# Unit 1's weights prepared in steps 1 to 5, the last unit's gates of five tiles given in its last three steps, and the sample's lane begun at the second output slot

## The chip, the cores and the metric

One Trainium2 chip, one of its cores. The metric is the device time of one execution in microseconds (us). The engines of the core are PE (TensorE, matmuls), DVE (VectorE), ACT (ScalarE), POOL (GpSimd) and SP (SyncE, which here only issues DMAs). Each takes its instructions in the order in which the program lists them for it, and an instruction that waits holds up what is listed behind it on its engine.

## What is computed

One layer of a streaming encoder: 2048 prompt rows (16 tiles of 128) and 128 sample rows (8 streams of 16) of width 1024 are normed and modulated to h; h times `w_in` gives queries, keys, values and two groups of gates; differential attention (softmax, 4 heads) and stick-breaking attention (8 heads) run side by side; their outputs are gated, projected, merged and projected again.

```python
def merge_branches(oa, ob, za, zb, ga, gb, subln_g, lam_init, w_branch_a, w_branch_b, w_out):
    b, s = oa.shape[:2]
    oa = rms_norm(oa, subln_g) * (1.0 - lam_init)
    ya = (oa.reshape(b, s, WIDTH_A) * jax.nn.silu(za)) @ w_branch_a
    yb = (ob.reshape(b, s, WIDTH_B) * jax.nn.silu(zb)) @ w_branch_b
    return (jax.nn.sigmoid(ga) * ya + jax.nn.sigmoid(gb) * yb) @ w_out
...
        h, gate = adaln_modulate(xp, c_prompt, norm_g[l], w_ada[l], b_ada[l])
        qa, ka, va, za, qb, kb, vb, zb, ga, gb = project_inputs(h, w_in[l], pos_p)
...
        xp = xp + gate * merge_branches(oa, ob, za, zb, ga, gb, subln_g[l], lam_init,
                                        w_branch_a[l], w_branch_b[l], w_out[l])
```

The sample rows do the same against a cache of 512 older keys and values. The new keys and values are outputs too.

## The kernel before

**Units, tiles, steps.** The heads are worked off in eight units. An even unit is one softmax head, an odd unit a pair of stick-breaking heads. Every unit goes over 17 tiles, the sample's tile (`NT`) first and then prompt tiles 0 to 15, so there are 136 steps `(u, t)`. All products that need more than half precision are made of f16 halves: h and each weight are cut into a high and a low half, and three matmuls stand for one.

**The main loop** (`for n in range(len(steps) + 2)`) gives the work of a step: score chunks of the step's tile against its keys (two matmuls of 128x512, L697 and L698), what ACT, DVE and POOL do to them (softmax for even units; for odd units the scan L671, which DVE runs over 512 columns at a time and the next chunk continues), the transposes of the weights by DMA (L615, issued on SP, into `wt`), and the products with the values (L754 to L759). Beside that stand pieces of the **projection line**, taken by `take(target)`: the projections run about five steps ahead of the scores (`LEAD`). `project` gives 24 matmuls L461 for a tile, and in the odd units 24 gate matmuls L537 more, all into the one bank "t" of PSUM; ACT takes the result out (L540) and SP stores it in `g_d`. The gate matmuls read the tile's h, which lies in one of three buffers `hs[0..2]` that `fetch_h` (L438) fills in turn from `hT_d`.

**Side pieces** of a step: `back`, the next unit's weights (`prepare_unit`: raw loads, sums of squares on ACT L295, a bound, then `cut` and `gate_cut` into halves, L315 on ACT or L317 on POOL and L320 on DVE); `spare`, sums of squares of the branch weights, the output weight and the cached values (a load of 512 KB and one L295 each); `cached`, keys of the cache. Unit 1 is the first one with gates. Its weights were begun at step 3 of unit 0.

**Early work** (`early_work`, from the end of the line on): the branch weights, then the inputs of the first two output tiles (`first`): o and z rows loaded into `hs[0]` and `hs[1]` (L1291, L1292), multiplied, cut into halves into `hs[2]` (L315, L320) and transposed on PE (L1281, taken out by ACT L1282).

**The output phase** has a slot n for each of the 17 tiles in the order 0 to 14, sample, 15, and two more. Slot n runs the branch projection L1471 of its n-th tile (48 matmuls) and the output projection L1508 of the tile before it (48), and prepares the tile after it. Beside them stands the **sample's lane**, the attention of the sample rows against their cache in 52 pieces, spread by `aside(n)` over the first 13 slots: loads `dc`, cast on ACT into `v16c` (L315), scores L849, weights through DMA into `dwt`, and L872.

A list scheduler orders the instructions of each engine from this program; those marked `kept` stay where the program has them.

## Time and profile before

| | us |
|---|---|
| median of 3 runs | 2244.19 |
| range of the runs | 2240.26 to 2244.84 |
| the profiled execution | 2238.37 |
| its span (first to last instruction) | 2236.6 |

The profiled execution's own time is 1.8 us above its span and 5.8 us below the median of the runs. In the span the main loop begins at about 130 us, its last score chunk is done at about 1774 us, and the output phase runs from about 1782 us to the end. The views used below are: the page (busy time of each engine), a table of windows (busy time of each engine in stretches of the span, with `PEclk`, the mean TensorE clock that was granted, 1.00 being full speed), groups of equal instructions (count, busy time, mean duration in ns, idle time of the engine just before them and what ended it), waits (what ended the idle time of an engine), and the timeline (start, duration, instruction, and in brackets the idle time ahead of it and its releaser). `PEld` is the loading of weights into the array, which overlaps PE.

### The profile page before, as it was taken

What the parts mean: (1) busy time and instruction counts of PE and PEld (TensorE: products, weight loads), DVE (VectorE), ACT (ScalarE), POOL (GpSimd) and SP (SyncE); (2) the same over time, 40 slices, a digit from 0 to 9 for tenths busy, and PEclk for the clock granted to TensorE, in tenths of its full rate; (3) what the DMA queues carried; (4) which work ended last, traced back from release to release, by engine and by line L of the source; (5) the groups of instructions that cost most, each with busy time, mean ns of one, the idle gap of its engine ahead of it and who ended that gap; (6) DMA issues with size and microseconds to landing.
All of it is one profiled execution on the core that took longest, in us unless ns stands there. A gap on an engine that the chain in (4) does not pass through costs nothing. (4 is left out here: it accounts for less than half of the span.)

```text
span 2236.6 us, 41454 instructions
## 1 busy us (share of the span) xinstructions
PE 2068.9 (93%) x14608; PEld 1115.8 (50%) x14608; DVE 1747.9 (78%) x3799; ACT 1606.9 (72%) x3212; POOL 700.4 (31%) x608
## 2 busy tenths in 40 slices
PE   5998999999999999999999998999998689999997
PEld 3654555555555455555544554555554334444443
DVE  4657868889887788988778888787778868888864
ACT  3967877789887778987677788876577666676531
POOL 1122014446420343752024356301334512211210
PEclk8999999999999999999999999999999699999999
DMA  9777768889797989978879899675667899899762
GB/s 331 257 247 177 168 153 208 198 212 208 194 248 163 226 205 199 213 209 215 198 191 222 187 219 207 188 165 130 148 154 170 168 254 267 230 247 241 194 170 66
DMA packets 824672, 450.00 MB, mean 201 GB/s; under 512 B 556081, under 2 KB 763233, under 8 KB 823950
## 3 DMA queue, kind: packets, MB, share of 16 engines
q1 hardware_dynamic: 823514, 446.96, 80.9%
q8 instruction: 114, 1.87, 0.3%
q14 instruction: 96, 0.79, 0.1%
q10 hardware_dynamic: 948, 0.39, 0.1%
HBM read 228.82 MB, written 86.02 MB: 141 GB/s over the span
## 5 line engine op out<-in xcount | busy, mean ns | idle before, releaser
L677 POOL TENSOR_TENSOR sc_p<-sc_p,sc_n 128x127 f32<-128x127 f32 (+7 forms) x192 | 313.2, 1634 | 663.9 <-DVE sc_n L671 514.1
L461 PEld LDWEIGHTS <-hs 128*128 128x128 f16 x3120 | 292.2, 98 | 312.4 <-issue 4.3
L461 PE MATMUL ps_mm<-wa,hs 128*128 128x512 f16 x1590 | 383.8, 380 | 1.5 <-DVE v L320 0.9
L461 PE MATMUL ps_mm<-wb,hs 128*128 128x512 f16 x1530 | 379.7, 379 | 1.0 <-DVE qbuf L496 1.0
L537 PE MATMUL ps_t<-wb,hs 128*128 128x512 f16 x1224 | 291.8, 379 | 3.2 <-DVE qst L565 2.9
L671 DVE TENSOR_TENSOR_SCAN sc_n<-ps_s,sc_n,zero_t 128x512 f32<-128x512 f32 x192 | 245.4, 1278 | 36.0 <-ACT ps_s L131 30.7
L697 PE MATMUL ps_s<-k,qst 128*128 128x512 f16 (+3 forms) x640 | 224.2, 351 | 38.8 <-DVE sc_n L671 26.8
L608 DVE TENSOR_TENSOR sc_n<-sc_p,sc_n 128x128 f16<-128x128 f32 (+7 forms) x192 | 221.8, 1157 | 39.7 <-ACT sc_n L605 39.2
L537 PEld LDWEIGHTS <-hs 128*128 128x128 f16 x1632 | 154.7, 98 | 182.6 <-DVE qst L565 7.3
L131 ACT ACTIVATE sc_p<-ps_s,usc 128x512 f32<-128x512 f32 (+3 forms) x320 | 203.2, 635 | 36.2 <-PE ps_s L698 22.6
L698 PE MATMUL ps_s<-k,qst 128*128 128x512 f16 (+3 forms) x640 | 225.0, 352 | 0.0
L605 ACT CAST sc_n<-sc_p 128x128 f16<-128x128 f32 (+7 forms) x192 | 154.8, 807 | 63.8 <-POOL sc_p L677 63.0
L131 ACT ACTIVATE ps_s<-ps_s,usc 128x512 f32<-128x512 f32 (+3 forms) x320 | 195.5, 611 | 0.0
L758 PE MATMUL ps_o<-v,wt 128*128 128x128 f16 x1088 | 135.5, 226 | 22.5 <-DMA wt<-sc_n 22.5
L1508 PE MATMUL ps_o<-wo,wb 128*128 128x512 f16 x624 | 142.3, 384 | 0.8 <-ACT wb L1282 0.8
L591 DVE TENSOR_SCALAR_CACHE_REDUCE sc_p<-ps_s,usc 128x512 f32<-128x512 f32 (+3 forms) x160 | 106.1, 664 | 31.8 <-PE ps_s L698 17.5
L758 PEld LDWEIGHTS <-wt 128*128 128x128 f16 x1088 | 103.1, 102 | 51.3 <-DMA wt<-sc_n 28.5
L759 PE MATMUL ps_o<-v,wt 128*128 128x64 f16 x1088 | 127.8, 199 | 0.0
L1517 POOL TENSOR_TENSOR x<-m,x 128x512 f32<-128x512 f32 x32 | 48.1, 1504 | 251.2 <-DVE m L1512 164.5
L671 DVE TENSOR_TENSOR_SCAN sc_n<-ps_s,zero_t 128x128 f32<-128x128 f32 (+3 forms) x128 | 104.2, 814 | 23.8 <-ACT ps_s L131 23.0
L502 POOL TENSOR_TENSOR rot<-pr,rope 128x256 f32<-128x256 f32 x68 | 56.7, 833 | 205.5 <-ACT pr L475 109.9
L754 PE MATMUL ps_o<-v,wt 128*128 128x128 f16 x544 | 101.5, 224 | 19.2 <-DMA wt<-sc_n 19.0
(379 smaller groups left out, 4547.9 us busy)
## 6 DMA issues: line engine op xcount, KB each, us to landing
hs<-hT_d SPq DMA_DIRECT2D x130, 512.0 KB, 4.6
g_d<-gt SPq DMA_DIRECT2D x68, 256.0 KB, 3.3
out_dram<-pr SPq DMA_DIRECT2D x204, 64.0 KB, 3.6
wa<-in_w_in_dram SPq DMA_DIRECT2D x34, 256.0 KB, 5.7
o_d<-o SPq DMA_DIRECT2D x136, 64.0 KB, 2.2
wa<-g_d SPq DMA_DIRECT2D x17, 512.0 KB, 4.7
wb<-g_d SPq DMA_DIRECT2D x17, 512.0 KB, 4.9
hs<-o_d SPq DMA_DIRECT2D x17, 512.0 KB, 4.5
```

Of the source, the lines that this page charges most:

```text
L131: i = S.activation(**kw)
L461: T.matmul(box["p"], box["h"][:, hi, k, :], U["w"][k][:, wi, :], start=(n == 0), stop=(n == 3 * KT - 1))
L537: T.matmul(box["g"][:, 0:gw], box["h"][:, hi, k, :], U["wg"][k // per][:, k % per, wi, :], start=(j == 0), stop=(j == 3 * KT - 1))
L605: x = S.copy(out=hi, in_=src)
L608: V.tensor_tensor(out=lo, in0=src, in1=hi, op=ALU.subtract)
L671: V.tensor_tensor_scan(out=dst[:, lo : lo + n][:, ::-1], data0=src[:, 0:n][:, ::-1], data1=zero_t[:, 0:1].to_broadcast([P, n]), initial=fi ...
L677: G.tensor_tensor(out=p[:, 0:m], in0=p[:, 0:m], in1=n[:, 1 : m + 1], op=ALU.mult)
L697: T.matmul(p[:, 0:n], qst[:, c, :], kk[:, c, 0:n], start=True, stop=False)
L698: T.matmul(p[:, 0:n], qst[:, 2 + c, :], kk[:, c, 0:n], start=False, stop=not diag)
L758: T.matmul(po[:, c * P : (c + 1) * P], wt[:, wj, :], vt[:, c, :, :], start=first, stop=False)
L759: T.matmul(po[:, c * P : c * P + 64], wt[:, nb + wj, :], vt[:, c, 0, :], start=False, stop=last)
L1508: T.matmul(po, st["y"][:, yi * 8 + k, :], wo[j * 4 + k // 2][:, wi, k % 2, :], start=(n == 0), stop=(n == 3 * KT - 1))
```

## The change

1. `prepare_unit(1)` begins at step 1 instead of 3, and its pieces are spread so that they end with step 5 instead of step 10. No sum of squares of `spare` is made in unit 0 any longer (nine were, in its last nine steps); they are made in unit 6.
2. The gate matmuls of tiles 11 to 15 of unit 7, the last one (5 x 24), leave the projection line. They are given as 60 pieces of two matmuls in the last three steps, in the order of tiles 13, 15, 14, 11, 12. The h of tiles 13, 14 and 15 is still in the three buffers; that of tiles 11 and 12 is loaded again, one after the other into `hs[2]`. `early_work` begins with the last two steps, where before it began as soon as the line was empty.
3. The sample's lane begins at slot 1; from there the 52 pieces are spread over 12 slots.
4. The output gate rows of the sample's tile come from `gate_rows(1, j)` (a load of 9x512 and one small matmul into bank "t") ahead of their multiplication; before, all were loaded at once and two matmuls L1503 put them into banks ahead of the tile's L1508. The norm and the store of the last two output tiles are given a little later in their slots.

```diff
--- before.py
+++ after.py
@@ -59,6 +59,9 @@
 H_AT = 2
 Q_BUFS = 6
 TR_AFTER = 5
+LATE, CUTS_AT = 5, 2
+LATE_ORDER = (NT - 3, NT - 1, NT - 2, NT - 5, NT - 4)
+LATE_SHARE = (0, 20, 20, 20)
 LEAD = 5.0
 TILE_TIME = 0.6
 SAMPLE_TIME = 0.3
@@ -431,6 +434,9 @@
         G.memset(qb[:, 1, :, 1, :], 0.0)
     silu_z = {}
     at_hand, ahead, fetched = {}, {}, []
+
+    def late(u, t):
+        return u == 7 and NT - LATE <= t < NT
 
     def fetch_h(u, t):
         ahead[u, t] = hs[len(fetched) % 3].bitcast(F16).rearrange("p (f k n) -> p f k n", f=2, n=P)
@@ -534,13 +540,18 @@
             for j in range(per * n, per * n + per):
                 hi, wi = ((0, 0), (0, 1), (1, 0))[j % 3]
                 k = j // 3
-                T.matmul(box["g"][:, 0:gw], box["h"][:, hi, k, :], U["wg"][k // per][:, k % per, wi, :], start=(j == 0), stop=(j == 3 * KT - 1))
+                x = T.matmul(box["g"][:, 0:gw], box["h"][:, hi, k, :], U["wg"][k // per][:, k % per, wi, :], start=(j == 0), stop=(j == 3 * KT - 1))
+                if late(U["u"], t) and j == per * n:
+                    kept(x)
             if per * n + per == 3 * KT:
                 gt = gts[:, 0:512]
-                S.activation(out=gt[:, 0:gw], in_=box["g"][:, 0:gw], func=AF.Identity, scale=sc[:, 6:7])
+                x = S.activation(out=gt[:, 0:gw], in_=box["g"][:, 0:gw], func=AF.Identity, scale=sc[:, 6:7])
+                if late(U["u"], t):
+                    kept(x)
                 load(out=g_d[t][:, g0 : g0 + gw], in_=gt[:, 0:gw])
 
-        return [lambda n=n: piece(n) for n in range(12)] + [lambda n=n: gate_piece(n) for n in range(3 * KT // per if gw else 0)]
+        U["gates", t] = box, [lambda n=n: gate_piece(n) for n in range(3 * KT // per if gw else 0)]
+        return [lambda n=n: piece(n) for n in range(12)] + ([] if late(U["u"], t) else U.pop(("gates", t))[1])
 
     def transpose_qk(U, t):
         g, i = t // 4, t % 4
@@ -986,7 +997,22 @@
                 fetch_h(*steps[m + 1])
             made[i]()
 
-        return [lambda i=i: piece(i) for i in range(12 + 3 * GATES[u][1] // 128)]
+        return [lambda i=i: piece(i) for i in range(12 + (0 if late(u, t) else 3 * GATES[u][1] // 128))]
+
+    def late_gates(t):
+
+        def piece(i):
+            box, made = units[7]["gates", t]
+            if i == 0 and t < NT - 3:
+                box["h"] = ahead[8, t]
+            made[i]()
+            if i == len(made) - 1:
+                j = LATE_ORDER.index(t) + 1
+                if 3 <= j < len(LATE_ORDER):
+                    ahead[8, LATE_ORDER[j]] = x = hs[2].bitcast(F16).rearrange("p (f k n) -> p f k n", f=2, n=P)
+                    load(out=x, in_=hT_d[LATE_ORDER[j] // 4][:, LATE_ORDER[j] % 4, :, :, :])
+
+        return [lambda i=i: piece(i) for i in range(3 * GATES[7][1] // 128)]
 
     starts = []
     for m in range(len(steps)):
@@ -1015,7 +1041,7 @@
         return out
 
     def norm_at(u, t):
-        return u < 7 and t < NT and (t >= 7 if u == 0 else t >= 9 or u == 6)
+        return u < 7 and t < NT and (t >= 16 if u == 0 else t >= 9 or u == 6)
 
     def keys_at(u, t):
         return u in (1, 3, 5) and t < 8 or u in (2, 4, 6) and 9 <= t < 13
@@ -1266,6 +1292,7 @@
     branch_weights = list(range(8))
 
     L = {}
+    behind = [fn for t in LATE_ORDER for fn in late_gates(t)]
 
     def cut(dst, st, src, k, j, s, n):
 
@@ -1392,11 +1419,11 @@
         if n < len(steps):
             u, t = steps[n]
             past += duration(t)
-            if t == (3 if u == 0 else NT) and u < 7:
+            if t == (1 if u == 0 else NT) and u < 7:
                 back += prepare_unit(u + 1)
             if u == 7 and not back and not spare and not cached and len(branch_weights) > 1:
                 side.append((1.0, branch_weight))
-            for fn in back[: -(-len(back) // max(1, (W_READY if u else W_READY + 2) - t % NT))]:
+            for fn in back[: -(-len(back) // max(1, (W_READY if u else 6) - t % NT))]:
                 side.append((1.0, back.pop(0)))
             for todo, here in ((spare, norm_at), (cached, keys_at)):
                 if todo and here(u, t):
@@ -1407,11 +1434,18 @@
                 qk = scores(units[u], t, made)
         target = position(len(steps) * past / whole + LEAD)
         pieces = take(target, min(n + 1, len(steps) - 1))
-        if at[0] == len(line) and not pieces and not spare and not cached:
-            if cuts is None:
-                cuts = early_work()
-            pieces = [(1.0, fn) for fn in cuts[: -(-len(cuts) // (len(steps) + 2 - n))]]
-            del cuts[: len(pieces)]
+        if at[0] == len(line) and not spare and not cached:
+            m = n - len(steps)
+            if behind:
+                k = -(-len(behind) * LATE_SHARE[m] // sum(LATE_SHARE[m:]))
+                pieces += [(1.0, fn) for fn in behind[:k]]
+                del behind[:k]
+            if m >= -CUTS_AT:
+                if cuts is None:
+                    cuts = early_work()
+                k = -(-len(cuts) // (len(steps) + 2 - n))
+                pieces += [(1.0, fn) for fn in cuts[:k]]
+                del cuts[:k]
             if n == len(steps) + 1:
                 while due and due[0][2] == 0.0:
                     due.pop(0)[3]()
@@ -1455,10 +1489,6 @@
             T.matmul(pg, sel[0:9, :] if i else ones[0:1, :], gsm[0:m, :], start=True, stop=True)
             return pg
 
-        def rows_of_gates():
-            L["gsm"] = dec.tile([P, NB, P], F32, tag="dc", name="gsm", bufs=4).rearrange("p b n -> p (b n)")
-            load(out=L["gsm"][0:9, :], in_=gate_d)
-
         def branches(st):
 
             def half(j, br):
@@ -1498,9 +1528,6 @@
                     load(out=box["x"], in_=x_rows(t))
                 x = box["x"]
                 c = slice(j * 512, (j + 1) * 512)
-                if t == NT:
-                    pg = bank("ts"[j])
-                    T.matmul(pg, sel[0:9, :], L["gsm"][0:9, c], start=True, stop=True)
                 po = bank("o")
                 n = 0
                 for yi, wi in ((0, 0), (0, 1), (1, 0)):
@@ -1512,7 +1539,7 @@
                     V.scalar_tensor_tensor(out=m, in0=po, scalar=st["f"][:, 1:2], in1=gate[:, c], op0=ALU.mult, op1=ALU.mult)
                 else:
                     S.activation(out=m, in_=po, func=AF.Identity, scale=st["f"][:, 1:2])
-                    V.tensor_tensor(out=m, in0=m, in1=pg, op=ALU.mult)
+                    V.tensor_tensor(out=m, in0=m, in1=gate_rows(1, j), op=ALU.mult)
                 if t != tiles[-1]:
                     G.tensor_tensor(out=x[:, c], in0=m, in1=x[:, c], op=ALU.add)
                     return
@@ -1572,17 +1599,13 @@
                 side += [(IN_AT[i], stage) for i, stage in enumerate(stages)]
             if n + 1 <= NT:
                 side += [(2, lambda n=n: turned(states[tiles[n + 1]], n + 1 >= MOVED)), (4.5, lambda n=n: opened(states[tiles[n + 1]]))]
-            if n <= NT and tiles[n] == NT:
-                side.append((3.3, rows_of_gates))
-            if n > NT:
-                side += [(0.6, lambda n=n: normed_rows(tiles[n - 2], boxes[n - 2])), (1.1, lambda n=n: stored_rows(tiles[n - 2], boxes[n - 2]))]
-            elif n > 1:
+            if n > 1:
                 side += [(1, lambda n=n: normed_rows(tiles[n - 2], boxes[n - 2])), (2.5, lambda n=n: stored_rows(tiles[n - 2], boxes[n - 2]))]
             if n <= NT:
                 side.append((4.4 if MOVED <= n < NT else 7, lambda n=n: turned_y(states[tiles[n]], MOVED <= n < NT)))
             order = [(i, 0, cost, fn) for i, (cost, fn) in enumerate(work)] + [(at - 0.5, i + 1, 0.9 if at == 7 or at == 2 and n + 1 < MOVED else 0.1, fn) for i, (at, fn) in enumerate(side)]
             work = [(cost, fn) for _, _, cost, fn in sorted(order, key=lambda e: e[:2])]
-            interleave(work, aside(n))
+            interleave(work, aside(n) if n else [])
 
 
 # ---- launch: one core; inputs and outputs as the reference has them ----
```

How the instructions move, at three places. (The change adds lines to the program: its L323 is L320 of before, L318 is L315, L626 is L615, L1318 and L1319 are the loads L1291 and L1292.)

DVE, where the gate weights of unit 1 are cut (`wa`/`wb` are weight buffers, `sg` their scale, `sc_p` and `sc_n` the softmax weights of a score tile), before:

```order
L641 TENSOR_TENSOR r<-r,ls_i 128x1
L646 SCALAR_TENSOR_TENSOR sc_p<-sc_n,r,sc_p 128x1024
L320 SCALAR_TENSOR_TENSOR wa_174<-wb_1430,sg,wa_174 128x2x512
L320 SCALAR_TENSOR_TENSOR wa_173<-wb_1431,sg,wa_173 128x2x512
L646 SCALAR_TENSOR_TENSOR sc_p<-sc_n,r,sc_p 128x128
L320 SCALAR_TENSOR_TENSOR k_2341<-rot,sq_711,k_2341 128x2x64
L496 SCALAR_TENSOR_TENSOR qbuf_214<-rot,sq_711,qbuf_214 128x2x64
L591 TENSOR_SCALAR sc_p,mx<-ps_s,usc_702 128x512
L591 TENSOR_SCALAR sc_n,mx<-ps_s,usc_702 128x512
L320 SCALAR_TENSOR_TENSOR sc_n<-sc_p,r,sc_n 128x1024
L591 TENSOR_SCALAR sc_p,mx<-ps_s,usc_702 128x512
L320 SCALAR_TENSOR_TENSOR wb_1430<-wb_1432,sg,wb_1430 128x2x512
```

and in the change:

```order
L323 SCALAR_TENSOR_TENSOR wa_176<-wb_1430,sg,wa_176 128x2x512
L650 RECIPROCAL r<-l 128x2
L651 SCALAR_TENSOR_TENSOR r<-l,r,nlam 128x1
L323 SCALAR_TENSOR_TENSOR wa_175<-wb_1431,sg,wa_175 128x2x512
L652 TENSOR_TENSOR r<-r,ls_i 128x1
L657 SCALAR_TENSOR_TENSOR sc_p<-sc_n,r,sc_p 128x768
L323 SCALAR_TENSOR_TENSOR wa_174<-wb_1432,sg,wa_174 128x2x512
L323 SCALAR_TENSOR_TENSOR wa_173<-wb_1433,sg,wa_173 128x2x512
```

The four cuts stood among the scores of the ninth tile of unit 0 (1024 + 128 columns), two of them on either side of it; now all four stand at its sixth (768 columns).

SP, in the last steps of unit 7 (`hs` are the three buffers of h, `wt` the transposed weights that PE waits for, `g_d` the stored gates, `o_d` and `z_d` what the first output tile loads), before:

```order
L1291 DMA hs_180<-o_d_62 128x1024
L541 DMA g_d_111<-gt_1421 128x512
L615 DMA_TRANSPOSE wt<-sc_n 128x16x128
L748 DMA o_d_73<-o 128x128
L615 DMA_TRANSPOSE wt<-sc_n 128x12x128
L615 DMA_TRANSPOSE wt<-sc_n 128x16x128
L615 DMA_TRANSPOSE wt<-sc_n 128x12x128
L748 DMA o_d_74<-o 128x128
L615 DMA_TRANSPOSE wt<-sc_n 128x16x128
L615 DMA_TRANSPOSE wt<-sc_n 128x14x128
```

and in the change:

```order
L551 DMA g_d_109<-gt_1421 128x512
L1319 DMA hs_181<-z_d_79 128x512
L626 DMA_TRANSPOSE wt<-sc_n 128x16x128
L626 DMA_TRANSPOSE wt<-sc_n 128x12x128
L626 DMA_TRANSPOSE wt<-sc_n 128x16x128
L551 DMA g_d_111<-gt_1421 128x512
L1318 DMA hs_180<-o_d_62 128x1024
L759 DMA o_d_74<-o 128x128
L626 DMA_TRANSPOSE wt<-sc_n 128x14x128
L1013 DMA hs_182<-hT_d_59 128x2048
L551 DMA g_d_110<-gt_1421 128x512
L626 DMA_TRANSPOSE wt<-sc_n 128x16x128
```

From the store of the last tile's gates on there were only transposes and stores of o; now five stores of gates, the two loads of the first output tile and two loads of h (L1013) stand among the transposes.

ACT, at the third output tile (`hs<-hs,suy` is the cut of an output tile's inputs, `v16c<-dc` the cast of the sample's cached values, `wo` the output weights), before:

```order
L315 ACTIVATE wo_22622<-x,s_w_19830 128x1024
L1282 COPY wb_1426<-ps_s 128x1024
L295 ACTIVATE junk,usq<-hs_180 128x1024
L315 ACTIVATE v16c<-dc,s_c 128x8x128
L1477 CAST wa_174<-wa_169 128x512
L315 ACTIVATE v16c<-dc,s_c 128x8x128 x2
L131 ACT_TABLE_LOAD
L131 ACTIVATE dsc,l<-dsc,nm 128x640 x2
L1477 CAST wa_174<-wb_1429 128x512
L131 ACT_TABLE_LOAD
L131 ACTIVATE hs_181<-hs_181 128x512
L315 ACTIVATE hs_182<-hs_180,suy 128x1024
```

and in the change:

```order
L298 ACTIVATE junk,usq<-hs_180 128x1024
L318 ACTIVATE wo_22634<-x,s_w_19830 128x1024
L1507 CAST wb_1429<-wb_1431 128x512
L318 ACTIVATE hs_182<-hs_180,suy 128x1024
L318 ACTIVATE v16c<-dc,s_c 128x8x128 x3
```

The cut of that tile stood behind three casts and two rows of the sample's softmax; now it stands ahead of them.

## The prediction

> **What bounds the kernel now.** I read the page first, for the engines over the whole span, then the table of windows, for where the engine with most work stands idle.
>
> ```profile
> PE 2068.9 (93%) x14608; PEld 1115.8 (50%) x14608; DVE 1747.9 (78%) x3799; ACT 1606.9 (72%) x3212; POOL 700.4 (31%) x608
> ```
>
> ```profile
> core 0: us, PE busy (x) PEld busy (x) DVE busy (x) ACT busy (x) POOL busy (x), PEclk, DMA share, GB/s
> 165.00:205.00 40.00, 39.56 (x243) 20.33 (x242) 29.24 (x84) 26.94 (x60) 10.81 (x13) 1.00 0.81 203
> 205.00:245.00 40.00, 26.54 (x183) 15.87 (x182) 34.10 (x100) 36.17 (x88) 7.79 (x9) 0.83 0.48 122
> 320.00:1600.00 1280.00, 1212.64 (x8635) 664.11 (x8634) 1055.74 (x2201) 1001.62 (x2144) 482.83 (x418) 0.99 0.85 199
> 1657.00:1722.00 65.00, 64.66 (x479) 34.95 (x478) 51.21 (x74) 48.95 (x98) 23.53 (x16) 1.00 0.77 163
> 1722.00:1774.00 52.00, 27.63 (x219) 16.24 (x215) 47.44 (x53) 39.00 (x63) 32.17 (x18) 0.72 0.71 138
> 1782.00:1835.00 53.00, 41.78 (x232) 19.57 (x233) 38.82 (x78) 31.89 (x40) 10.25 (x7) 0.89 1.01 263
> 1835.00:1890.00 55.00, 50.55 (x400) 24.38 (x398) 41.02 (x90) 34.48 (x50) 11.91 (x9) 0.96 1.05 257
> ```
>
> PE sets the pace nearly everywhere (93%; 94.7% from 320 to 1600 us). It stands still in three places: 13.5 us in 205 to 245, 24.4 us in 1722 to 1774, 15.7 us in the first two stretches of the output phase, at a lowered clock in each. The parts of the change lie in just these three.
>
> **The change part by part.** *A, unit 1's weights.* What PE waits for in 205 to 245 us, and then what the weights and the moved sums cost on ACT and DVE (groups in 165 to 205 and 205 to 245 us):
>
> ```profile
> PE ps_o L754 <- DMA wt<-sc_n: 7.0, 3, 5.0
> PE ps_t L537 <- ACT qst L565: 2.5, 1, 2.5
> ```
>
> ```profile
> L295 ACT ACTIVATE junk<-wb 128x1024 f16<-128x1024 f32 x4 | 4.2, 1049 | 0.0
> L315 ACT ACTIVATE wb<-wa,sw 128x512 f16<-128x512 f32 x4 | 2.5, 705 | 0.0
> L295 ACT ACTIVATION_READ_ACCUMULATOR junk<-wb 128x1 f32 x4 | 0.8, 188 | 0.0
> L320 DVE SCALAR_TENSOR_TENSOR wb<-wa,sw,wb 128x512 f16<-128x512 f32 x8 | 6.4, 841 | 0.7 <-POOL wb L317 0.7
> ```
>
> ```profile
> L295 ACT ACTIVATE junk<-wa,g 128x1024 f16<-128x1024 f32 x3 | 3.4, 1142 | 0.0
> L315 ACT ACTIVATE wb<-wb,sg 128x1024 f16<-128x1024 f32 x2 | 2.3, 1140 | 0.0
> L315 ACT ACTIVATE wa<-wb,sg 128x1024 f16<-128x1024 f32 x1 | 1.1, 1140 | 0.0
> L295 ACT ACTIVATION_READ_ACCUMULATOR junk<-wa,g 128x1 f32 x3 | 0.6, 194 | 0.0
> L320 DVE SCALAR_TENSOR_TENSOR wb<-wb,sg,wb 128x1024 f16<-128x1024 f32 x2 | 2.6, 1288 | 0.0
> L320 DVE SCALAR_TENSOR_TENSOR wa<-wb,sg,wa 128x1024 f16<-128x1024 f32 x2 | 2.5, 1280 | 0.0
> ```
>
> In 205 to 245 the bound is not PE but ACT (36.2 of 40 us) and DVE (34.1), which make the softmax that PE's transposed weights come from. Over 165 to 245 ACT has 63.1 us of work. It loses 7.5 (squares, cuts of w), 4.0 (three sums, 3.4 + 0.6) and 3.4 (gate cuts), so 48.2 are left; DVE's 63.3 lose 6.4 and 5.1, so 51.8. PE needs 39.6, and 26.5 x 0.83 = 22.0 at full clock: 61.6 of the 80. So the bound goes back to PE, and at most 18.4 us can be won. PE's rows up to unit 1's first gates are the same matmuls, scores and value products only listed earlier among the projections, so the stretch before takes them up while PE keeps busy. Not all goes: softmax chains of that length stay. I take two thirds, **-12**; ends -3 (only the wait for qst, 2.5 us, goes) and -18. The nine sums come back in unit 6: 9 x (1.14 + 0.19) = 12.0 us of ACT where it is busy 78% of the time. They are hidden there by PE (94.7%); without that cover they would cost a part of PE's idle share, 5.3%. I take **+1**; ends 0 and +5.
>
> *B, late gates.* The gate matmuls of 1657 to 1722 us, one of them in the timeline, and what ends PE's idle time in 1722 to 1774:
>
> ```profile
> L537 PE MATMUL ps_t<-wb,hs 128*128 128x512 f16 x90 | 21.9, 379 | 0.3 <-DVE sc_n L670 0.3
> L537 PE MATMUL ps_t<-wa,hs 128*128 128x512 f16 x30 | 7.5, 379 | 0.0
> ```
>
> ```profile
> 1672.71 2.75 PE L537 MATMUL ps_t<-wb,hs 128*128 128x512 f16 x12
> 1675.30 0.19 PE L759 MATMUL ps_o<-v,wt 128*128 128x64 f16 x1
> ```
>
> ```profile
> PE ps_s L697 <- DVE sc_n L671: 13.2, 12, 2.7
> PE ps_o L758 <- DMA wt<-sc_n: 9.4, 6, 3.8
> ```
>
> Twelve matmuls take 2.59 us to the next row, 0.216 each, so 120 take 25.9 us. All 120 lie where PE is full; the change puts them where it idles for 24.4 us waiting for DVE's scan and for transposes. Then PE needs 92.3 of these 117 us, and DVE, 51.2 + 47.4 = 98.7, becomes the bound. In 1722 to 1774, where DVE is the bound now, it is 91% busy. At that density 98.7 become 108.2: **-8.8**. The five loads of h become seven, and one 512 KB load takes 4.6 us to landing:
>
> ```profile
> hs<-hT_d SPq DMA_DIRECT2D x130, 512.0 KB, 4.6
> ```
>
> Ends: 0, when half of the gates (13 us) stands in front of a score that the scan waits for, which eats the gain; and -14, at a DVE density of 96%.
>
> *C, the sample from slot 1 on.* Waits of PE in 1782 to 1890 us, and the place of the longest:
>
> ```profile
> PE ps_s L1281 <- ACT hs L315: 8.9, 2, 6.6
> PE ps_t L872 <- DMA dwt<-dsc: 4.4, 2, 3.2
> ```
>
> ```profile
> 1829.12 1.03 PE L1281 MATMUL ps_s<-id,hs 128*128 128x128 f16 x8 [6.58 <-ACT hs L315]
> ```
>
> ```profile
> 1814.29 1.15 ACT L315 ACTIVATE v16c<-dc,s_c 128x1024 f16<-128x1024 f32 x1 [3.14 <-DMA dc<-in_cache_a_v_dram]
> 1819.20 1.15 ACT L315 ACTIVATE v16c<-dc,s_c 128x1024 f16<-128x1024 f32 x1 [3.25 <-DMA dc<-in_cache_a_v_dram]
> 1821.38 1.15 ACT L315 ACTIVATE v16c<-dc,s_c 128x1024 f16<-128x1024 f32 x1 [1.03 <-DMA dc<-in_cache_a_v_dram]
> ...
> 1827.93 1.13 ACT L315 ACTIVATE hs<-hs,suy 128x1024 f16<-128x1024 f32 x1
> ```
>
> ACT waits 7.4 us for three loads of the sample with the third tile's cut queued behind them; in the change the cut comes first. The stall of 6.6 us goes, and part of the lowered clock (0.11 x 41.8 = 4.6) with it, but the lane now runs five pieces per slot and not four, in slots whose DMA share is already 1.0. I take **-6**; ends -11 (the idle time of 1782 to 1835) and +4, when the 4.4 us for `dwt` come once more.
>
> *D, the sample's gate rows.*
>
> ```profile
> 2195.91 1.12 PE L1503 MATMUL ps_t<-gsm,sel 9*128 9x512 f32 x2
> 2207.42 1.12 PE L1503 MATMUL ps_s<-gsm,sel 9*128 9x512 f32 x2
> ```
>
> The same two matmuls run a few matmuls later; the multiplication waits for them while PE has the last tile's L1508 to do. **0**; ends 0 and +1.1, one of them exposed. The later norms and stores are covered by the last slot's matmuls.
>
> **The sum**: -12 + 1 - 8.8 - 6 = -25.8. From the profiled execution's 2238.4 this gives 2212.6; it lies 5.8 below the median of the runs, and on the scale of the runs, 2244.2, I forecast **2218 us**.
>
> **The rivals.** *R1, B brings nothing because DVE already sets the pace in 1657 to 1722.* For it: DVE is 79% busy there, 98.7 us of the 117 are its own, and its scans form a chain. Against it: PE has 0.3 us idle in 65 at full clock. Without B the sum is -17, 2227. The Trainium skill, "Perfetto Trace Analysis", section "Identifying the Most-Contended Engine", says that matmul busy time misjudges PE and that the share of weight loads should be used. By that rule PE would be at 54% (34.95 of 65) and DVE the engine to relieve, which is this rival. The 0.216 us per matmul and the granted clock of 1.00 speak against it here.
>
> *R2, A brings little.* Unit 1's gates still stand behind the same scores and value products, and the softmax chain of the tile that they follow may itself be the wait (the 7.0 us for `wt`). With A at its end of -3: -17, 2227.
>
> *R3, the change doesn't do what it says.* The late gates merely fill gaps that DVE's chain keeps open, the sample's lane pays back in slots 1 to 4 what slot 0 wins, and A is at its end: -3 + 1 + 0 + 0 = -2, 2242, no change.
>
> *R4, slower: SP's queue in the last steps.* Nine rows now stand among the transposes that wait, directly or through ACT, for late gates: five stores, two loads of the first output tile into h's buffers, two reloads into one buffer. What is queued behind each is a transpose, and behind that PE's value products and, through the scores' buffers, the scan. Such waits in SP's queue, 1650 to 1790 us before:
>
> ```profile
> SPq L615 <- DVE sc_n L608: 35.6, 16, 4.6
> ...
> SPq L615 <- PE ps_t L537: 4.4, 1, 4.4
> ...
> SPq L438 <- PE ps_t L537: 2.0, 1, 2.0
> ```
>
> At 4.4 us each, nine cost 39.6; with B's gain gone the sum is -17 + 39.6 = +23, 2267. It decides against the change from six such waits on (26 us). Against it: a tile's gates are only 24 x 0.216 = 5.2 us of PE, and SP waits 35.6 us for what DVE hands to the transposes, so it has slack ahead of most of them. The Trainium skill, "DMA: Bandwidth & Descriptors", section "Anatomy of one DMA — SWDGE (gpsimd) path", says that a DMA's wait is served on the issuing sequencer before dispatch, which is this rival's mechanism; the last two rows above agree, as waits of the queue's own.
>
> *R5, the output phase is bound by DMA* (share 1.01 and 1.05 in its first 108 us): the lane in 12 slots costs 4 instead of winning 6: -16, 2228.
>
> **How the numbers follow.** About 0.2%, 4.5 us, is what a measurement of this kernel can tell from no change. Chances: forecast 0.48, R1 0.13, R2 0.12, R3 0.09, R4 0.10, R5 0.08. The likeliest case alone runs from 2206 to 2230 (A, B and C halfway to their ends). Upwards the range takes in R1, R2 and R5 and stops short of R3 and R4: 2205 to 2240. Faster: forecast, R1, R2, R5 and a little of R3, 0.84; same: most of R3, 0.06; slower: R4, 0.10.
>
> **What would show it.** A right: in 205 to 245 us, PE idle below 5 us and its clock near 1.0, gate cuts before 190 us. B right: no gates ahead of the last three steps, PE idle between unit 7's last projection and the first L1471 below 8 us, DVE above 90%; wrong, and R4 right, if SP's waits for L543 (the gates' new line) add up to over 20 us and PE waits longer for `wt`. C right: no wait of several us at L1281 in slots 0 to 2; R5 if those of L872 grow. The forecast fails if the end of the scores (1774) comes less than 12 us earlier, or if the output phase gets longer.

## The result and the profile after

| | median, us | range of the runs, us | ratio to before, 95% interval |
|---|---|---|---|
| before | 2242.65 | 2237.54 to 2244.84 (6 runs) | |
| the change | 2219.45 | 2213.60 to 2225.32 (6 runs) | 0.9898, 0.9876 to 0.992 |
| the change again (e1) | 2223.29 | 2218.65 to 2229.53 (6 runs) | 0.9915, 0.990 to 0.993 |

The change is faster by 15.7 to 27.8 us, taking both comparisons. Three executions are left out of the ratios below as slow, one of e4 (2753 us) and two of e11 (7547 and 7590 us). The profiled execution of the change took 2225.32 us (span 2223.5), the slowest of its six, while that of before was one of its fastest: these two traces differ by 13.1 us only, and no reading below rests on that difference alone. All microseconds worked out from a ratio below are (ratio - 1) x 2242.65.

The page of the change, busy times of the engines:

```profile
PE 2061.2 (93%) x14608; PEld 1110.4 (50%) x14608; DVE 1743.8 (78%) x3799; ACT 1606.2 (72%) x3212; POOL 699.6 (31%) x608
```

The same windows of the change as in the prediction; then the first slots of its output phase, 1766 to 1817 us for 1782 to 1835 before, and 1817 to 1870 for 1835 to 1890:

```profile
165.00:205.00 40.00, 37.53 (x252) 20.10 (x251) 32.56 (x98) 31.74 (x74) 12.79 (x14) 1.00 0.89 217
205.00:245.00 40.00, 35.86 (x265) 20.07 (x263) 34.05 (x102) 31.63 (x77) 3.64 (x5) 0.96 0.51 111
320.00:1600.00 1280.00, 1212.44 (x8627) 662.95 (x8626) 1058.36 (x2197) 1008.71 (x2156) 484.99 (x419) 0.99 0.87 202
1657.00:1722.00 65.00, 55.10 (x424) 30.37 (x423) 62.25 (x85) 55.08 (x106) 30.00 (x20) 0.92 0.77 158
1722.00:1774.00 52.00, 39.09 (x303) 22.45 (x302) 41.82 (x68) 34.91 (x53) 25.35 (x16) 0.87 0.89 204
1766.00:1817.00 51.00, 44.58 (x269) 21.86 (x267) 39.82 (x78) 28.60 (x35) 10.44 (x9) 0.96 1.01 281
1817.00:1870.00 53.00, 47.12 (x315) 22.09 (x313) 40.14 (x93) 36.22 (x54) 12.34 (x9) 0.97 1.08 252
```

In 205 to 245 us PE works 35.9 us and not 26.5, at a clock of 0.96 and not 0.83; in 1657 to 1722 DVE is at 96% and PE has room. Where the time went is seen best by the start of the same instruction in each trace. The table takes matmuls by their number among those of their line (from the records of the traces, line numbers as in the kernel before) and gives the difference to before, in us. At all places but two the matmuls ahead on PE are as many as in before, to within 3: no. 433 has 44 more ahead of it in the change, e1 and e3, and the one of slot 4 has 24 fewer in the change and e1.

| place (time before) | the change | e1 again | e3 part 1 | e4 gates | e9 sums | e10 lane |
|---|---|---|---|---|---|---|
| L461 no. 121 (104.7), ahead of the main loop | +1.0 | +1.0 | +0.3 | -1.5 | -1.5 | -0.3 |
| L461 no. 433 (199.8), unit 1 | +9.9 | +9.7 | +8.8 | -1.5 | -1.2 | -0.3 |
| L537 no. 46 (267.8), unit 1 | -9.0 | -9.3 | -11.5 | -2.0 | -4.0 | +0.4 |
| L461 no. 865 (495.4), unit 2 | -9.5 | -10.9 | -11.9 | -2.4 | -9.4 | +0.1 |
| L461 no. 2730 (1408.7), unit 6 scores | -9.0 | -11.9 | -13.6 | +5.6 | -10.7 | +10.1 |
| L697 no. 542 (1496.1), unit 6 scores | -2.5 | -6.7 | -8.5 | +5.4 | -3.9 | +9.6 |
| L461 no. 3145 (1641.3), unit 7 scores | -6.6 | -10.3 | -12.1 | +5.5 | -7.4 | +9.4 |
| first L1471 (1782.1) | -15.5 | -19.8 | -11.6 | -4.1 | -8.1 | +9.2 |
| L1471 of slot 4 (1897.5) | -23.3 | -26.6 | -15.2 | -5.2 | -8.2 | -0.3 |
| L1471 of slot 8 (2000.5) | -16.3 | -20.9 | -13.3 | +0.8 | -6.2 | +8.7 |
| last L1508 (2225.7) | -12.9 | -19.6 | -11.3 | +0.9 | -5.3 | +10.8 |

Each column is one execution (e4's was its slowest but the one left out, e10's its second slowest), so its last row is not the gain of the run; the differences from row to row are what is read.

The change is 10 us behind at the 433rd projection, mostly because that one now stands behind scores and value products that were listed later before; at no. 46 of L537 and at the start of unit 2, where the order is the same again, it is 9 to 10 us ahead. In the change and e1 5 to 7 are lost in unit 6 and 4 of it won back by unit 7, some 9 come in unit 7's last steps, some 7 in slots 0 to 4, and these 7 to 10 are gone again by the end.

### The profile page after: what moved, and what is told of

Its sections match the earlier page's. It is cut to its first block, busy times and chain, and to the rows that moved or that the text cites. A ratio compares the mean times of both kernels' runs of the same rounds, so it can differ in the third digit from the quotient of the medians.

```text
span 2223.5 us, 41495 instructions
## 1 busy us (share of the span) xinstructions
PE 2061.2 (93%) x14608; PEld 1110.4 (50%) x14608; DVE 1743.8 (78%) x3799; ACT 1606.2 (72%) x3212; POOL 699.6 (31%) x608
## 5 line engine op out<-in xcount | busy, mean ns | idle before, releaser
L467 PE MATMUL ps_mm<-wa,hs 128*128 128x512 f16 x1590 | 391.2, 382 | 5.3 <-DMA hs<-hT_d 5.0
L543 PE MATMUL ps_t<-wa,hs 128*128 128x512 f16 x1020 | 242.3, 380 | 2.1 <-DVE qst L576 2.0
L543 PE MATMUL ps_t<-wb,hs 128*128 128x512 f16 x612 | 151.7, 383 | 4.8 <-DMA hs<-hT_d 2.1
L769 PE MATMUL ps_o<-v,wt 128*128 128x128 f16 x1088 | 135.2, 224 | 22.1 <-DMA wt<-sc_n 21.9
L1501 PEld LDWEIGHTS <-wa 128*128 128x128 f16 x816 | 77.7, 98 | 94.2 <-issue 4.1
```

Source lines behind the costliest of these rows:

```text
L467: T.matmul(box["p"], box["h"][:, hi, k, :], U["w"][k][:, wi, :], start=(n == 0), stop=(n == 3 * KT - 1))
L543: x = T.matmul(box["g"][:, 0:gw], box["h"][:, hi, k, :], U["wg"][k // per][:, k % per, wi, :], start=(j == 0), stop=(j == 3 * KT - 1))
L769: T.matmul(po[:, c * P : (c + 1) * P], wt[:, wj, :], vt[:, c, :, :], start=first, stop=False)
```

## The experiments

**The parts apart.** e1 is the changed kernel unedited:

> The changed kernel once more, unedited, for a second profile and more times. The first profile was of its slowest execution (2225.3 of 2213.6 to 2225.3) and shows the output phase 2.6 us longer than before, with 11.2 us of waits for dwt where before had 5.2. Theory 1 (the lane squeezed into 12 slots gives back what slot 0 wins, in every execution): the same waits for dwt, 9 us or more, in the second profile, and the output phase again as long as before or longer. Theory 2 (the executions differ in just these waits): a profile of a faster execution, under 2219, shows under 6 us of them and an output phase 3 to 8 us shorter than before.

Measured: 2223.29, ratio 0.9915. Its profile is of an execution of 2218.7 us, with an output phase of 444.2 us (start of the first L1471 to the end of the last L1508), as long as before's 443.9; the first profile has 446.5. The waits of PE for `dwt` in the output phase, of before, of the change and of e1, one line each:

```profile
PE ps_t L872 <- DMA dwt<-dsc: 5.2, 4, 3.2
```

```profile
PE ps_t L883 <- DMA dwt<-dsc: 11.3, 7, 3.1
```

```profile
PE ps_t L883 <- DMA dwt<-dsc: 8.5, 6, 2.6
```

The count is nearly theory 1's 9 us: in a faster execution too the phase is no shorter. This execution lies ahead of the first one's by 0 to 5 us from unit 1 to slot 8 and by 6.7 at the end.

e2 puts the lane back to slot 0 (`interleave(work, aside(n) if n else [])` becomes `interleave(work, aside(n))`):

> The changed kernel with the sample's lane from slot 0 again (four pieces a slot). If the later lane wins 6 us as the forecast has it, this is 6 us slower than the change (about 2225). If it gives back in slots 4 to 8 what it won in slots 1 to 3, this is within 3 us of the change (2216 to 2222) and its profile shows a stall of 5 us or more at the cut of the second or third output tile and under 6 us of waits for dwt. If the later lane costs, this is faster than the change by 2 us or more.

Measured: 2223.27, ratio 0.9911 (0.9898 to 0.9924), to be compared with e1's 2223.29 on the same chip. The lane's later start brings nothing. The stall that it removes is there again, and the waits for `dwt` are smaller, in e2's output phase:

```profile
PE ps_s L1308 <- ACT wa L1309: 6.0, 1, 6.0
PE ps_t L883 <- DMA dwt<-dsc: 6.0, 5, 2.7
```

e10 makes this part alone, in the kernel before:

> The kernel before with the sample's lane from slot 1 alone. The forecast's term is -6. With the rest of the change in place the lane's start made no difference (e2: 2223.3 with it at slot 0, 2223.3 at slot 1). Theory 1 (the phase is bound by DMA up to its fifth slot or so, so what slot 0 wins is paid back): within 2 us of before, slots 1 to 3 ahead of it by 5 us or more and nothing left of that by slot 8. Theory 2 (before still has a stall to remove that the rest of the change removed otherwise): 4 us or more faster than before.

Measured: 2244.68, ratio 1.0015 (1.0002 to 1.0028), so 0.4 to 6.3 us slower. By the table 9.5 us are won from slot 0 to slot 4 and 9.0 lost by slot 8. The waits of PE in its output phase, where before had 8.9 for `hs` and 5.2 for `dwt`:

```profile
PE ps_t L872 <- DMA dwt<-dsc: 13.3, 8, 3.7
PE ps_s L1281 <- ACT hs L315: 2.4, 1, 2.4
```

6.5 us less of one wait, 8.1 more of the other: an exchange, as theory 1 has it, though the time lies somewhat above its 2 us. The traces fall apart by the lane's start alone: in the five with the lane at slot 0 (before, e2, e3, e4, e9) PE waits 8.2 to 11.2 us at L1281 and 4.4 to 7.7 for `dwt`, in the eight with it at slot 1 and all cached values read, 0 to 6.4 and 8.4 to 13.8.

e3 is part 1 alone:

```diff
-            if t == (3 if u == 0 else NT) and u < 7:
+            if t == (1 if u == 0 else NT) and u < 7:
...
-            for fn in back[: -(-len(back) // max(1, (W_READY if u else W_READY + 2) - t % NT))]:
+            for fn in back[: -(-len(back) // max(1, (W_READY if u else 6) - t % NT))]:
...
-        return u < 7 and t < NT and (t >= 7 if u == 0 else t >= 9 or u == 6)
+        return u < 7 and t < NT and (t >= 16 if u == 0 else t >= 9 or u == 6)
```

> The kernel before with part 1 alone (unit 1's weights in steps 1 to 5, the nine sums of squares moved to unit 6). By the forecast's terms -12 + 1: 2231.6. By the trace of the change -10 by 300 us and +3 to +4 in unit 6: 2236. If the stall of 205 to 245 us is the softmax chain itself and not the weights (the rival R2): 2240 or more.

Measured: 2230.72, ratio 0.995 (0.993 to 0.997), -11.2 us (-6.7 to -15.7).

e4 is the late gates with the sample's gate rows, without part 1 and with the lane at slot 0:

> The kernel before with the late gates of five tiles (and the sample's gate rows from gate_rows), without part 1 and with the lane from slot 0. By the forecast -8.8: 2233.8. If DVE set the pace in 1657 to 1722 us anyway (R1): 2241 to 2244. If SP's queue pays for the nine rows among the transposes (R4): over 2247.

Measured: 2235.37, ratio 0.9962 (0.9948 to 0.9975), -8.5 us (-5.6 to -11.7); in its trace -9.6 us between L461 no. 3145 and the first L1471.

**Part 1 taken apart.** e9 makes the third edit of e3 alone, e5 makes all of the change but that one:

> The kernel before with one condition changed: no sums of squares in unit 0, the nine made in unit 6; unit 1's weights as before in steps 3 to 10. With the weights moved and the sums left in unit 0 (e5) the trace stood 2 to 3 us ahead of before at the end of unit 1's projections, with both moved 8 to 11. Theory 1 (ACT is the bound of 205 to 245 us and every piece taken from it counts, so the two add up): the sums alone bring 5 to 8 us by that place, and 2236 to 2240 in the end, since unit 6 pays some 4. Theory 2 (both have to go, since the later of them keeps the stall): within 2 us of before at that place and 2244 or more in the end.

> The changed kernel with the nine sums of squares back in unit 0 (its last nine steps); unit 1's weights still in steps 1 to 5. The forecast gave A -12 as a whole and +1 for the nine sums in unit 6. Theory 1 (the weights' earlier time alone brings A, the sums matter little): within 3 us of the change, and unit 6 without the loss of 5 to 9 us between its ninth and last tile that the profiles of the change show. Theory 2 (ACT is so full in 205 to 245 us that the three sums there count): 4 us or more slower than the change, the stall of 205 to 245 us back in part.

Measured: e9 2234.92, ratio 0.9967 (0.9954 to 0.998), -7.4 us; e5 2237.66, ratio 0.9969 (0.9955 to 0.9983), -7.0 us, some 12 to 16 slower than the change.

At the start of unit 2 (L461 no. 865), less the value at L461 no. 121, e9 stands at -7.9, e5 at -3.0 + 0.3 = -2.7, both parts together at -10.5 (the change) to -12.2 (e3). So by that place the sums alone bring most of part 1, against what the forecast had credited, and the weights alone little; by the end the runs show nothing for the weights alone, for e5's -7.0 is no better than e4's -8.5, which has neither. Closer behind the stall the picture is another: at L537 no. 46 (267.8 us) e9 stands at -2.5, e5 at -3.4 + 0.3 = -3.1 and both together at -10.0 to -11.8, so neither alone removes the stall. The 5.4 us that e9 wins from there to unit 2 are not in the traces with both, which win 0.4 to 1.6 there (the change, e1, e3); why e9 wins them is open.

The window 205 to 245 us of before is in the prediction (PE 26.5 at 0.83); in e9, in e5, and with both above:

```profile
205.00:245.00 40.00, 28.95 (x205) 17.11 (x204) 34.40 (x90) 31.77 (x75) 6.67 (x8) 0.87 0.54 121
```

```profile
205.00:245.00 40.00, 31.70 (x213) 18.93 (x212) 31.45 (x91) 31.41 (x78) 3.72 (x4) 0.83 0.50 116
```

In this stretch the two add up, with something over: 2.4 us more of PE with the sums gone, 5.2 with the weights gone, 9.3 with both. But moving the weights has a price before it that the sums have not. Window 120 to 200 us of before, of e9 and of the change:

```profile
120.00:200.00 80.00, 79.56 (x481) 41.74 (x480) 50.62 (x150) 50.99 (x115) 22.23 (x29) 1.00 0.79 218
```

```profile
120.00:200.00 80.00, 79.61 (x481) 41.45 (x478) 52.42 (x152) 53.73 (x126) 22.93 (x29) 1.00 0.73 203
```

```profile
120.00:200.00 80.00, 76.15 (x467) 40.29 (x466) 58.33 (x173) 58.27 (x133) 26.16 (x30) 1.00 0.73 209
```

ACT and DVE take in 7 to 8 us of work there and PE, which was full, loses 3.4.

**The sums in other places.** e6 lets units 1 to 5 take them from tile 7 on (`t >= 9 or u == 6` becomes `t >= 7 or u == 6`); e12 gives two a step to units 1, 3 and 5 and one to 2, 4 and 6, from tile 9 on:

```diff
-        return u < 7 and t < NT and (t >= 16 if u == 0 else t >= 9 or u == 6)
+        return (0 if u in (0, 7) or t == NT or t < 9 else 2 if u % 2 else 1)
...
-                    for _ in todo[: -(-len(todo) // left)]:
+                    for _ in todo[: -(-len(todo) * int(here(u, t)) // left)]:
```

> The changed kernel with the sums of units 1 to 5 from tile 7 on and not from tile 9 on, so that none of the nine is left for unit 6 (four sums there and not fourteen). If unit 6 pays for the sums (a net +3 to +4 between its ninth tile and unit 7's ninth in three of four profiles) and units 1 to 5 have room, this is 3 us faster than the change or more. If units 1 to 5 pay the same, within 2 us of it.

> The changed kernel with the sums spread by weight: two a step in tiles 9 to 15 of units 1, 3 and 5 (stick-breaking, where ACT has fewer and DVE more to do), at most one in those of units 2, 4 and 6, and none in unit 6 before its ninth tile. If unit 6's loss of 4 to 9 us comes from the number of its sums, this is 3 us or more faster than the change. If the place of the sums disturbs the order of a unit wherever they are (as in e6, which lost 17 us in unit 2 and 11 in unit 4), it is slower than the change by 3 us or more.

Measured: e6 2245.23, ratio 1.0002 (0.9988 to 1.0016): the whole gain is gone. e12 2237.13, ratio 0.997 (0.9957 to 0.9984). Both expectations of a gain failed. Against before, at places with the same order on PE, e6 loses 11.5 us between 495 and 786 us, most of it in unit 2's scores, and 6.0 between 1011 and 1263 us (from the middle of unit 4's scores to the middle of unit 5's; the expectation above has 11 in unit 4); e12 loses 9.1 between 495 and 674 us and 11.9 between 916 and 959 us, at the end of unit 3's. In e6, PE's longest wait there, from its timeline:

```profile
638.12 0.29 PE L765 MATMUL ps_o<-v,wt 128*128 128x128 f16 x1 [5.85 <-DMA wt<-sc_n]
```

Such waits, for transposed weights, sum up to 13.1 us in 480 to 680 us of e6 and to 5.8 in the same window of the change. What sets them apart in order is open: these kernels list much else differently too.

Unit 6 in the change shows the same wait and what stands around it. From PE's timeline, SP's timeline (issues, in order), and a table of windows with the DMA share in the last column but one:

```profile
1465.73 0.29 PE L765 MATMUL ps_o<-v,wt 128*128 128x128 f16 x1 [5.61 <-DMA wt<-sc_n]
```

```profile
1452.35 0.53 SPq L959 DMA_DIRECT2D keys_bk<-wb  x1
1452.93 0.42 SPq L931 DMA_DIRECT2D wa<-in_cache_b_v_dram  x1
1453.45 0.99 SPq L759 DMA_DIRECT2D o_d<-o  x1
1454.53 0.46 SPq L931 DMA_DIRECT2D wb<-in_cache_b_v_dram  x1
...
1458.36 4.50 SPq L626 DMA_TRANSPOSE wt<-sc_n  x1
1462.95 0.53 SPq L959 DMA_DIRECT2D keys_bk<-wb  x1
1463.57 1.55 SPq L626 DMA_TRANSPOSE wt<-sc_n  x1
```

```profile
1455.00:1460.00 5.00, 5.00 (x49) 3.09 (x46) 4.71 (x12) 4.29 (x11) 2.15 (x1) 1.00 1.00 279
1460.00:1465.00 5.00, 0.12 (x1) 0.00 (x0) 2.79 (x11) 2.99 (x11) 0.00 (x0) 0.81 1.37 116
1465.00:1470.00 5.00, 4.27 (x30) 3.22 (x31) 0.59 (x1) 0.00 (x0) 0.00 (x0) 0.51 1.00 305
```

Among the nine issues ahead of a transpose stand two loads for the moved sums (L931, 512 KB each) and a store of the cache's keys; the DMA engines are full for 15 us, PE does 0.12 us of work in five, and after it runs at half clock. The Trainium skill, "DMA: Bandwidth & Descriptors", section "Issuing engines are not separate DMA queues", says that DMAs issued by ScalarE, SyncE or GpSimd end up on the same 16 DMA engines and interleave there. The issues shown here are all SP's; the window shows those engines full, and not the interleaving.

ACT stands still for 8.0 us at the same place (for nothing that the profile shows). All eight traces with the nine sums in unit 6 (the change, e1, e2, e3, e7, e8, e9, e11) have this stall of ACT, 4.5 to 8.0 us, and at the same place a wait of PE of 3.1 to 5.6; before, e4, e5, e6, e10 and e12, without them, have no such stall. So the nine sums bring it, but that it comes from their loads is read from the place alone: no run moved the loads without ACT's work, and sums made in unit 6 before its key stores begin were not tried. From L461 no. 2730 to L697 no. 542 the eight lose 3.2 to 6.8 us and by L461 no. 3145 they win 3.5 to 4.4 of it back. They do so in spite of a second wait, in unit 7's first tiles, for a load of h; it is the 5.0 us in this line of the change's page (a group of equal matmuls over the whole span), and ends at 1568.9 us:

```profile
L467 PE MATMUL ps_mm<-wa,hs 128*128 128x512 f16 x1590 | 391.2, 382 | 5.3 <-DMA hs<-hT_d 5.0
```

All ten traces whose sums have left unit 0 have it, 4.3 to 5.6 us, and the four others have none.

**Late gates: how many.** e7 and e11 take three tiles (no load of h repeated) and four (one repeated):

```diff
-LATE, CUTS_AT = 5, 2
-LATE_ORDER = (NT - 3, NT - 1, NT - 2, NT - 5, NT - 4)
-LATE_SHARE = (0, 20, 20, 20)
+LATE, CUTS_AT = 3, 2
+LATE_ORDER = (NT - 3, NT - 1, NT - 2)
+LATE_SHARE = (0, 12, 12, 12)
```

(e7; e11 has `LATE` 4, `NT - 4` as the last of the order, and shares of 16.)

> The changed kernel with the late gates of tiles 13, 14 and 15 alone (36 pieces, 12 in each of the last three steps), whose h is still in the buffers: no load of h is repeated. 48 gate matmuls (10.4 us) go back to the stretch where PE is full. Theory 1 (each late tile is worth its 5.2 us of PE up to what DVE leaves free): the scores end some 4 us later than in the change, the time 2 to 5 us above it. Theory 2 (the two reloads into one buffer cost what their tiles win: in the change PE waits 2.1 us for them, and ACT and DVE then 2.8 each for PE's scores): within 2 us of the change or faster.

> The changed kernel with late gates of tiles 12 to 15 alone (48 pieces, 16 in each of the last three steps), so one load of h is repeated and not two. Three late tiles (e7) were 3.3 us slower than the change, each on the time of before on its chip. Theory 1 (each of the two reloaded tiles is worth the same): 1 to 2 us slower than the change. Theory 2 (the second reload into the one buffer costs what its tile wins): as fast as the change or up to 2 us faster.

Measured: e7 2227.02, ratio 0.9925 (0.9909 to 0.9941); e11 2226.68, ratio 0.9925 (0.991 to 0.994); the change 0.9898 and 0.9915. Five tiles are as good or better, but the intervals overlap. From L461 no. 3145 to the first L1471 the traces win 6.9 us with three tiles, 9.9 with four (where 16 fewer matmuls stand ahead of that L1471), 8.9 and 9.5 with five in the change and e1; but all eight traces with five tiles spread from 6.0 to 9.6, so these single executions do not tell three tiles from five, and show no gain from the fifth. What stands against such a gain, in the waits of PE and of SP's queue in the change, 1650 to 1767 us:

```profile
PE ps_o L769 <- DMA wt<-sc_n: 11.4, 7, 3.7
PE ps_s L708 <- DVE sc_n L682: 9.1, 13, 2.2
PE ps_t L543 <- DMA hs<-hT_d: 2.1, 2, 1.3
```

```profile
SPq L626 <- DVE sc_n L619: 22.2, 13, 4.0
...
SPq L626 <- PE ps_t L543: 1.7, 1, 1.7
...
SPq L1013 <- PE ps_o L770: 0.7, 1, 0.7
```

PE waits 2.1 us for the repeated loads, and ACT 2.8 us for the scores behind one of them (its timeline at 1738.8). SP's queue hardly waits for late gates: 1.7 us.

**Less DMA in the output phase.** e8 reads only half of the cached values:

```diff
-            load(out=vc, in_=values_by_block[nv][:, j, :, h * P : (h + 1) * P])
+            load(out=vc[:, 0:4, :], in_=values_by_block[nv][:, j, 0:4, h * P : (h + 1) * P])
...
+            for b in (0, 4):
+                split(v16[:, b : b + 4, 0, :], v16[:, b : b + 4, 1, :], vc[:, 0:4, :], sv, S)
```

The casts take the four blocks that were read twice over, in two pieces, so this kernel leaves half of the cached values out of the sample's attention.

> The changed kernel with the sample's cached values loaded by half: each load dc brings 4 of its 8 blocks (256 KB and not 512), and the cast reads these four twice, so half of the cached values are not read. 8.4 MB less in the output phase, with PE's work unchanged and ACT's and DVE's casts in two pieces. Theory 1 (R5: the output phase is bound by DMA in its first five slots, and the lane's waits for dwt come from there): the waits for dwt fall under 4 us, the output phase gets 5 us shorter or more, and the kernel comes to 2215 or less. Theory 2 (the lane's own chain or PE's order sets the phase): within 3 us of the change.

Measured: 2219.34, ratio 0.9887 (0.987 to 0.9904), beside e5 to e7 on the same chip. Its output phase takes 438.2 us, the shortest of all fourteen traces; the others lie between 443.9 and 450.6. The waits for `dwt` are 6.7 us and not under 4, and the median is not 2215 or less, so these parts of theory 1's expectation failed; by the medians e8 lies within theory 2's 3 us of the change's first measurement, and its interval overlaps both of the change's. So the one trace speaks for a phase shortened by less DMA and the times do not confirm it; the share that goes through `dwt` is not settled either.

## Why the forecast came out

The forecast was 2218, the median 2219.45. The sum held because its two large terms held; one term of 6 us was wrong, and the first comparison came out 4 us better than the second, which hides that: the hit to within 1.5 us is in part luck. By the parts measured apart, -11.2 - 8.5 and 0 to +3 for the lane, the change is worth 16 to 20 us; the direct comparisons say 22.9 and 19.1.

- **A with its return in unit 6** (forecast -12 + 1): -11.2 by e3 (-6.7 to -15.7). The signs came true: in 205 to 245 us PE idles 4.1 us at a clock of 0.96, and the gate cuts are done by 181 us. The account behind it held in part. The prediction credited the three sums with 4.0 of the 14.9 us of ACT that it took out of 165 to 245 us, and let the stretch before take the weights in at no cost. At 268 us the sums alone are worth 2.5 us, the weights alone 3.1 and both 10.0 to 11.8, so they are not shares of one total: the stall goes when both go. By unit 2 the sums alone are worth 7.9, and this the prediction has nowhere. PE pays 3.4 us in 120 to 200 us for the weights, which "PE keeps busy" had excluded.
- **+1 for the nine sums in unit 6** (ends 0 and +5): from L461 no. 2730 to no. 3145 the eight traces with them change by -1.2 to +3.3 us, seven of them by +1.5 or more; e4, e5 and e10, without them, by -0.7 to +1.4. So the size held, as far as single traces tell. Its reason, time of ACT hidden by PE, did not: the sums bring a stall, and what makes up for most of it is the stretch behind, for which the runs give no cause.
- **B** (forecast -8.8): -8.5 by e4, and -6.0 to -9.6 between L461 no. 3145 and the first L1471 in the eight traces with five late tiles. DVE became the bound as the sum had it, 62.3 of 65 us busy. That rules R1 out: 120 matmuls taken from PE do shorten the stretch. The Trainium skill, "Perfetto Trace Analysis", section "Identifying the Most-Contended Engine", has the room left on PE judged by the FLOPs done against the peak (MFU) and by the share of weight loads; the second alone, at 54%, called PE far from its bound, and the run decides against it. The signs named for it did not come true: PE still idles 22.6 us (86.1 - 63.6) between unit 7's last projection and the first L1471, where before had 27.8 in 71.4, and DVE is 86% busy in that stretch (74.0 of 86.1), not over 90%. The gain lies in the stretch ahead of it, which got shorter.
- **R4** did not happen: nine rows in SP's queue, 1.7 us of waits of transposes for late gates, and 1.8 of a store for ACT's copy of them, against the 4.4 each that the rival supposed.
- **C** (forecast -6): 0 by e1 against e2, +0.4 to +6.3 by e10. The stall at L1281 fell as predicted; the step that failed is that the time would be kept: what slots 0 to 3 win is lost again by slot 8 (9.5 and 9.0 us in e10). R5 is what happened in its outcome, an exchange of one wait for another, though at 0 and not at its +4; that a full DMA is the cause (share 1.01 and 1.08 in the first slots) is argued, with e8's trace for it.
- **D** (0): from slot 16's first L1471 to the end the change and e1 differ by 0.2 us from before.
- **R2** fell in its form (the stall of 205 to 245 us went), but is true of the weights alone, which leave most of that stall standing (8.3 us of idle PE in e5's 205 to 245 us, 13.5 before). R3, no change, is ruled out by both intervals.
- **The range and the signs**: A, B and C halfway to their ends add up to 2210 to 2232, and not to the 2206 to 2230 of the prediction. One of its two signs of failure came true without the forecast failing: the output phase got longer, 446.5 and 444.2 us against 443.9, while unit 7's last scan ends 17 and 21 us earlier.

## What to carry to other kernels

Price a moved piece by what stands around its new place, and not by its own time alone: the nine small sums in unit 6 leave the gain standing, and all sums from tile 7 on in units 1 to 5 (e6) take the whole of it. Before comparing one instruction's start in two traces, compare what stands ahead of it. Work of the full engine is worth moving into a stretch where another engine's chain leaves it idle, about up to the second engine's own total. A stall removed in a stretch whose DMA engines are full can come back later in that stretch, as the lane's did; look there before counting it.

## What the runs showed of the hardware

One place in unit 4 has a wait that differs between executions, with the same order of instructions. Before and e10 are the same kernel up to the output phase; the first line is from before's PE timeline, the second from e10's, the same matmul:

```profile
968.25 0.23 PE L758 MATMUL ps_o<-v,wt 128*128 128x128 f16 x1 [2.28 <-DMA wt<-sc_n]
```

```profile
975.65 0.23 PE L758 MATMUL ps_o<-v,wt 128*128 128x128 f16 x1 [3.82 <-DMA wt<-sc_n]
```

Here PE waits 1.5 us longer for a transpose and is 3.2 us further behind by the next projections, with a window of granted clock 0.66 behind it in e10. The change, e1, e2 and e4 lose 3 to 4.5 us at the same place; before and e3 lose none, e9 0.7. The executions of one kernel lie 2.5 to 16 us apart in these comparisons (4 to 24 of each), often more than a part of the change is worth, so one profile of each kernel does not tell such parts apart; how much of that spread is this one wait is open.
